# Weight sums one product ahead of the cast that reads them, raw weight tiles of a pair loaded earlier, and the eight parts of z loaded side by side, in a hybrid state-space and attention layer

## The chip, the cores and the metric

The kernel runs on one core of a Trainium2 chip. The metric is the device time of one execution in microseconds (us), as the median over runs. In the traces PE is TensorE (matmuls), DVE is VectorE, ACT is ScalarE, POOL is GpSimd, and SP is SyncE, which here only issues DMAs.

## The reference, cut to what matters

One layer: a projection of 528 tokens (512 and 16 meta tokens), a state-space branch, an attention branch, then sigmoid gates that mix the branches, an output product and a layer norm. The change touches the products of the gates and the entry of the GLU product of the state-space branch:

```python
hf = h.astype(jnp.float32)                                  # 528 x 2048
...
z = jax.nn.gelu(y)                                          # state-space branch, width 1024
hg = z @ w_glu.astype(jnp.float32) + b_glu.astype(jnp.float32)
return hg[..., :SSM_WIDTH] * jax.nn.sigmoid(hg[..., SSM_WIDTH:])
...
gates = jax.nn.sigmoid(hf @ w_gate[layer].astype(jnp.float32) + b_gate[layer].astype(jnp.float32))
mixed = gates[..., :D_MODEL] * y_ssm + gates[..., D_MODEL:] * y_sb
```

## The kernel before

All large products are made in three passes: each float32 operand is split into a high half (a cast on ACT) and a low half (source less high half, a subtraction on DVE, `split_lo`), and `mm3` issues high by high, high by low and low by high. In the trace the high halves of a weight tile are called `whi`, the low halves `wlo`, and a raw tile is 128 x 1024 float32 (512 KB).

Weights go through a pipeline of three functions that count factors. `load_upto` issues the DMA of raw tiles on SP, `prep_upto` makes `whi` and `wlo`, and `slot` runs one factor's matmuls. `slot` for factor c first runs what is left of the product before (`pend`), prepares factors up to c + 2, and then writes eight pieces of three matmuls; ahead of the sixth piece it issues loads up to factor c + 5. Fillers (`schedule`) are pieces of other work that `run_fillers` puts in at a given count of pieces. The order is the order in which this Python runs: the program is recorded under `manual_schedule`, each engine takes its own instructions in that order, and semaphores hold an instruction until its inputs are there and its output buffer is free. `whi` and `wlo` have three buffers each, so those for product x + 2 take the place of those of product x - 1.

**The gates** are made in 16 pairs (`pair(j)`), one for 128 columns of each of the two gates. A pair has four raw tiles, `11`, `12`, `21`, `22` (gate one or two, first or second half of the 2048 input rows), and is computed with seven products in place of eight (Strassen's scheme in Winograd's form): sums of the raw tiles are multiplied with sums of quarters of the input (`T1`, `T2`, `T3`, `t4`, made ahead). Products are numbered 0 to 6 here; their factors are `11`, `s2`, `s1`, `21` (overwritten by 11 - 21), `12`, `s2` (overwritten by 12 - s2) and `22`, with s1 = 21 + 22 and s2 = s1 - 11. The sums are DVE instructions of 128 x 1024. In the kernel before `factor` writes a sum at the place where its product's factor is prepared, right ahead of the cast that reads it; s1 and s2 both stand ahead of the cast for product 1. A product is 24 matmuls of 256 columns. The products accumulate into three PSUM tiles a, b, c; `e0` to `e6` add them up on DVE and apply the sigmoid on ACT, each written at the start of the next slot. b takes products 1, 3 and 6; `e1` reads b after product 1 (`u2`, b + p1), so product 3 can't start before that addition is done.

The raw tiles `11`, `21` and `12` share three buffers, and `22` has two of its own. `11`, `21` and `22` of a pair are issued together, at product 2 of the pair before, and `12` at product 3; what really holds each is its buffer, which the pair before has to release.

**The entry of the GLU product.** z lies in DRAM as eight parts of 128 x 512 (`zd`, 256 KB each). Their high and low halves `zh` and `zl` are needed by all 16 products of the GLU, part kk by piece kk. `load_z(j)` is a filler that issues the DMA into `zt` (one buffer), the cast to `zh` and the subtraction to `zl`; eight of them are placed three pieces apart, from product 4 of the last pair on. Their place in memory is that of `T1` to `T3`, which product 3 of the last pair reads last.

## Time and profile before

| | |
|---|---|
| median of 3 runs | 1505.92 us (1505.59 to 1507.81) |
| the profiled execution, its own time | 1507.89 us |
| its span, first to last instruction | 1506.1 us |
| PE busy | 1440.1 us, 96% |
| DVE busy | 942.0 us, 63% |
| ACT busy | 482.0 us, 32% |
| mean granted clock of PE | 0.988 of full |

The span is what the trace covers; 1.8 us of the execution's own time lie around it. Matmuls are pipelined: one of 256 columns is shown 0.28 us long, but starts follow each other every 0.12 us, so a gap is read from the starts of neighbours. The idle time that a view puts before a matmul is counted from the modelled end of the one before, and is shorter than the delay of its start.

### The profile page before, as it was taken

To read this page: it belongs to the slowest core of one execution; us is meant where nothing else is said; L and a number is where in the kernel's file an instruction comes from. 1 tells how busy PE (TensorE), PEld (TensorE's weight loads), DVE (VectorE), ACT (ScalarE), POOL (GpSimd) and SP (SyncE) were. 2 spreads that over 40 slices of the span, in tenths; PEclk is the share of its full clock that TensorE was granted. 3 is DMA by queue.
4 is the path that set the end of the run, shared out by engine and by line. 5 is a ranking of instruction groups with operands and counts; after the bars stand their busy time and mean duration, and the time that the engine had idled before them with its cause. 6 is when DMAs were issued, how large, how long until landed. Compare 5 with 4: busy or idle time off the path is not lost.

```text
span 1506.1 us, 22031 instructions
## 1 busy us (share of the span) xinstructions
PE 1440.1 (96%) x9040; PEld 1295.2 (86%) x9040; DVE 942.0 (63%) x1397; ACT 482.0 (32%) x764; POOL 48.8 (3%) x95
## 2 busy tenths in 40 slices
PE   7999999999999999998999999996999999999996
PEld 7989999999999898887999999995788888888885
DVE  8887767666767677577666666664454444423357
ACT  5322323233232323234444444433332222221120
POOL 0830000000000000000000000000000000000000
PEclk9999999999999999999999999998899999999998
DMA  7345253434434343462333233233454444474323
GB/s 250 117 129 142 85 141 96 135 105 118 126 114 107 113 116 118 122 219 92 121 131 125 100 133 133 95 124 120 160 150 151 141 151 134 136 208 153 98 98 112
DMA packets 96357, 196.50 MB, mean 130 GB/s; under 512 B 28416, under 2 KB 41984, under 8 KB 95488
## 3 DMA queue, kind: packets, MB, share of 16 engines
q1 hardware_dynamic: 77552, 177.20, 38.5%
q10 hardware_dynamic: 18704, 17.90, 3.5%
q8 instruction: 71, 1.16, 0.3%
q14 instruction: 30, 0.25, 0.1%
HBM read 172.78 MB, written 22.28 MB: 130 GB/s over the span
## 4 chain that ended last, share of the span: by engine, by line
PE 67%; DVE 17%; ACT 8%; issue 5%; DMA 2%; ACTq 0%; SPq 0%; DVEq 0%
PE acc L177 18%; PE acc L178 18%; PE acc L179 18%; ACT whi L171 6%; DVE wlo L96 5%; DVE s L96 4%; PE aux L177 3%; PE aux L179 2%; PE aux L178 2%; DVE u L96 2%; DVE raw L96 1%; DMA zt<-zd 1%; PE aux L818 1%; PE aux L779 1%; PE aux L814 1%
## 5 line engine op out<-in xcount | busy, mean ns | idle before, releaser
L177 PE MATMUL acc<-Xh,whi 128*128 128x256 f32 (+2 forms) x1664 | 520.9, 313 | 6.7 <-ACT whi L277 4.6
L96 DVE TENSOR_TENSOR wlo<-raw,whi 128x1024 fp32r<-128x1024 f32 (+1 forms) x242 | 294.9, 1220 | 362.6 <-ACT whi L171 355.4
L178 PE MATMUL acc<-Xl,whi 128*128 128x256 f32 (+2 forms) x1664 | 515.0, 309 | 2.3 <-DVE Xl L96 2.2
L179 PE MATMUL acc<-Xh,wlo 128*128 128x256 f32 (+2 forms) x1664 | 514.0, 309 | 0.0
L171 ACT CAST whi<-raw 128x1024 fp32r<-128x1024 f32 x238 | 247.7, 1049 | 463.6 <-PE acc L178 311.0
L177 PEld LDWEIGHTS acc<-Xh,whi 128*128 128x128 f32 x1664 | 316.3, 190 | 22.3 <-ACT whi L277 4.6
L178 PEld LDWEIGHTS acc<-Xl,whi 128*128 128x128 f32 x1664 | 316.0, 190 | 17.2 <-DVE Xl L96 3.5
L179 PEld LDWEIGHTS acc<-Xh,wlo 128*128 128x128 f32 x1664 | 315.6, 190 | 15.5
L96 DVE TENSOR_TENSOR wlo<-s,whi 128x1024 fp32r<-128x1024 f32 x48 | 58.8, 1225 | 69.8 <-ACT whi L171 69.8
L171 ACT CAST whi<-s 128x1024 fp32r<-128x1024 f32 x48 | 50.3, 1048 | 89.0 <-DVE s L96 81.5
L177 PE MATMUL acc<-zh,whi 128*128 128x512 f32 x128 | 53.2, 416 | 13.4 <-ACT zh L1180 7.8
L177 PE MATMUL acc<-T3h,whi 128*128 128x256 f32 x128 | 37.4, 292 | 17.4 <-DVE u L96 17.4
L178 PE MATMUL acc<-zl,whi 128*128 128x512 f32 x128 | 52.9, 413 | 0.3 <-DVE zl L96 0.2
L179 PE MATMUL acc<-zh,wlo 128*128 128x512 f32 x128 | 52.2, 408 | 0.0
L179 PE MATMUL acc<-oh,wlo 128*128 128x512 f32 x128 | 49.8, 389 | 0.0
L178 PE MATMUL aux<-wlo,mh 128*128 128x512 f32 x128 | 49.8, 389 | 0.0
L177 PE MATMUL aux<-whi,mh 128*128 128x512 f32 x128 | 49.8, 389 | 0.0
L179 PE MATMUL aux<-whi,ml 128*128 128x512 f32 x128 | 49.8, 389 | 0.0
L178 PE MATMUL acc<-wlo,mh 128*128 128x512 f32 x128 | 49.8, 389 | 0.0
L178 PE MATMUL acc<-sl,whi 128*128 128x512 f32 x128 | 49.8, 389 | 0.0
L178 PE MATMUL acc<-ol,whi 128*128 128x512 f32 x128 | 49.8, 389 | 0.0
L179 PE MATMUL acc<-sh,wlo 128*128 128x512 f32 x128 | 49.8, 389 | 0.0
(274 smaller groups left out, 2310.1 us busy)
## 6 DMA issues: line engine op xcount, KB each, us to landing
raw<-wst SPq DMA_DIRECT2D x238, 512.0 KB
gt<-gtd SPq DMA_DIRECT2D x32, 256.0 KB
xb<-xT SPq DMA_DIRECT2D x16, 264.0 KB
X<-brep SPq DMA_DIRECT2D x8, 512.0 KB
X<-pvd SPq DMA_DIRECT2D x16, 256.0 KB
X<-sd SPq DMA_DIRECT2D x8, 512.0 KB
gtd<-ga ACTq DMA_DIRECT2D x16, 256.0 KB
gtd<-gb ACTq DMA_DIRECT2D x16, 256.0 KB
```

The lines of the kernel that those rows point to most:

```text
L96: eng.tensor_tensor(out, a, b, op)
L171: A.copy(h, t)
L177: PE.matmul(o, ah, bh, start=start, stop=False, **kw)
L178: PE.matmul(o, ah, bl, start=False, stop=False, **kw)
L179: PE.matmul(o, al, bh, start=False, stop=stop, **kw)
L779: PE.matmul(vp[:, g, 0:NK], W["vt"][:, g].rearrange("p r q -> p (r q)"), ut[:, g * NK:g * NK + NK], start=True, stop=True,)
L814: PE.matmul(yp[:, g, 0:SK], W["ot"][:, g].rearrange("p t c -> p (t c)"), hs[:, g * NK + MK - 1:g * NK + MK - 1 + SK], start=True, stop=False,)
L818: PE.matmul(yp[:, g, 0:SK], W["mt"][:, g, :], ut[:, g * NK + MK:g * NK + MK + SK], start=False, stop=True,)
```

## The change

The sums move out of the function that picks a factor. `sums_upto` writes them one product ahead: while factor i is prepared, after its cast and before its low half, it writes the sum that belongs to factor i + 1 (s1 with factor 0, s2 with factor 1, 11 - 21 with factor 2, 12 - s2 with factor 4). `prep_upto` then picks the tile by the table `FACTOR`. The loads of a pair are issued earlier and in another order: `11` and `22` at factor 5 of the pair before (`load_first`), `21` at factor 6 (`load_second`), `12` at factor 1 as before. `load_z` only issues the DMA, into one of eight `zt` buffers, all eight at the start of product 4 of the last pair; `split_z` has the cast and the subtraction, from piece 10 on, two pieces apart. The later loads of `gd`, which use the same tag, get the eight buffers too.

```diff
             else:
-                c = GATES + 4 * pr[0]
-                w = sev.setdefault(pr[0], {})
-                if pr[1] == 0:
-                    w["11"], w["21"] = load_raw(c), load_raw(c + 2)
-                    w["22"] = load_raw(c + 3, sev["p"], "r22", bufs=2)
-                elif pr[1] == 1:
+                n_, x = pr
+                c = GATES + 4 * n_
+                w = sev.setdefault(n_, {})
+                nx = sev.setdefault(n_ + 1, {})
+                if i == GATES:
+                    load_first(w, c)
+                    load_second(w, c)
+                if x == 1:
                     w["12"] = load_raw(c + 1)
+                elif x == 5 and n_ < NSEV - 1:
+                    load_first(nx, c + 4)
+                elif x == 6 and n_ < NSEV - 1:
+                    load_second(nx, c + 4)
...
-    def factor(w, x):
...
+    def load_first(w, c):
+        w["11"] = load_raw(c)
+        w["22"] = load_raw(c + 3, sev["p"], "r22", bufs=2)
+
+    def load_second(w, c):
+        w["21"] = load_raw(c + 2)
+
+    summed = [GATES]
+
+    def sums_upto(f):
+        while summed[0] <= min(f, GATES + 7 * NSEV - 1):
+            n_, x = pair_of(summed[0])
+            w = sev[n_]
+            if x == 0:
+                w["s1"] = sev["p"].tile([P, 1024], F32, tag="s1", name="s1")
+                tt(w["s1"], w["21"], w["22"], ALU.add)
+            elif x == 1:
+                w["s2"] = sev["p"].tile([P, 1024], F32, tag="s2", name="s2")
+                tt(w["s2"], w["s1"], w["11"], ALU.subtract)
+            elif x == 2:
+                tt(w["21"], w["11"], w["21"], ALU.subtract)
+            elif x == 4:
+                tt(w["s2"], w["12"], w["s2"], ALU.subtract)
+            summed[0] += 1
+
+    FACTOR = ("11", "s2", "s1", "21", "12", "s2", "22")
...
-            t = raws.pop(i) if pr is None else factor(sev[pr[0]], pr[1])
+            t = raws.pop(i) if pr is None else sev[pr[0]][FACTOR[pr[1]]]
...
             A.copy(h, t)
+            if GATES - 1 <= i + 1:
+                sums_upto(i + 1)
             split_lo(lo, t, h)
...
-            t = zst["p"].tile([P, S], F32, tag="zt", bufs=1, name="zt")
+            t = zst["p"].tile([P, S], F32, tag="zt", bufs=NT, name="zt")
             SP.dma_start(out=t, in_=zd[j])
+            zst["t", j] = t
+
+        def split_z(j):
+            t = zst.pop(("t", j))
             A.copy(zst["h"][:, j, :], t)
             split_lo(zst["l"][:, j, :], t, zst["h"][:, j, :])
...
-                    schedule([(0, open_z)] + [(1 + 3 * k, lambda k=k: load_z(k)) for k in range(NT)])
+                    schedule([(0, open_z)] + [(0, lambda k=k: load_z(k)) for k in range(NT)]
+                             + [(10 + 2 * k, lambda k=k: split_z(k)) for k in range(NT - 1)] + [(23, lambda: split_z(NT - 1))])
...
-            hold["t2"] = tmpl("zt")
+            hold["t2"] = tmpl("zt", NT)
```

How the instructions stand on DVE from the sum s1 of a pair on, before the change (`raw_7105`, `raw_7107` and `raw_7109` are tiles 11, 21 and 22; `p1`, `u2` and `u3` are the additions of `e6`, `e1` and `e3`):

```order
L96 TENSOR_TENSOR s1_7219<-raw_7107,raw_7109 128x1024
L96 TENSOR_TENSOR s2_7220<-s1_7219,raw_7105 128x1024
L96 TENSOR_TENSOR wlo_7224<-s2_7220,whi_7223 128x1024
L96 TENSOR_TENSOR p1_7049<-p1_7049,acc_7013 128x256
L96 TENSOR_TENSOR wlo_7258<-s1_7219,whi_7257 128x1024
L96 TENSOR_TENSOR raw_7107<-raw_7105,raw_7107 128x1024
L96 TENSOR_TENSOR wlo_7289<-raw_7107,whi_7288 128x1024
L96 TENSOR_TENSOR u2_7316<-acc_7252,p1_7285 128x256
L96 TENSOR_TENSOR wlo_7319<-raw_7142,whi_7318 128x1024
L96 TENSOR_TENSOR s2_7220<-raw_7142,s2_7220 128x1024
L96 TENSOR_TENSOR wlo_7354<-s2_7220,whi_7353 128x1024
L96 TENSOR_TENSOR u3_7384<-acc_7252,p1_7285 128x256
```

The same stretch on DVE with the change (`raw_7041`, `raw_7078` and `raw_7043` are tiles 11, 21 and 22; `raw_6798` is tile 22 of the pair before):

```order
L96 TENSOR_TENSOR s1_7161<-raw_7078,raw_7043 128x1024
L96 TENSOR_TENSOR wlo_7159<-raw_6798,whi_7158 128x1024
L96 TENSOR_TENSOR s2_7193<-s1_7161,raw_7041 128x1024
L96 TENSOR_TENSOR wlo_7191<-raw_7041,whi_7190 128x1024
L96 TENSOR_TENSOR u2_7089<-u2_7089,acc_7015 128x256
L96 TENSOR_TENSOR raw_7078<-raw_7041,raw_7078 128x1024
L96 TENSOR_TENSOR wlo_7224<-s2_7193,whi_7223 128x1024
L96 TENSOR_TENSOR p1_7054<-p1_7054,acc_7014 128x256
L96 TENSOR_TENSOR wlo_7259<-s1_7161,whi_7258 128x1024
L96 TENSOR_TENSOR s2_7193<-raw_7142,s2_7193 128x1024
L96 TENSOR_TENSOR wlo_7293<-raw_7078,whi_7292 128x1024
L96 TENSOR_TENSOR u2_7323<-acc_7253,p1_7290 128x256
```

Each sum now stands one low half earlier than the low half that is made of it: s1 ahead of the low half of the pair before's factor 22, s2 ahead of that of 11, 11 - 21 ahead of that of s2, and 12 - s2 ahead of that of 11 - 21.

On SP around the loads of z, before the change (`DMAHW` is a DMA's semaphore, `DVE`, `PE`, `Pool` and `Activation` those of engines):

```order
L123 DMA raw_10588<-wst 128x1024 [waits DMAHW4_49,DVE_49]
L1179 DMA zt_10617<-zd0_90 128x512 [waits PE_49]
L1179 DMA zt_10630<-zd1_91 128x512 [waits DMAHW6_49,DMAHW5_49,DVE_49]
L123 DMA raw_10637<-wst 128x1024 [waits DMAHW7_49,DMAHW0_49]
L1179 DMA zt_10645<-zd2_92 128x512 [waits DMAHW6_49,DVE_49]
L1179 DMA zt_10664<-zd3_93 128x512 [waits DMAHW1_49,DMAHW0_49,DVE_49]
```

And with the change:

```order
L123 DMA raw_10588<-wst 128x1024 [waits DVE_49]
L1194 DMA zt_10614<-zd0_90 128x512 [waits DMAHW5_49,PE_49]
L1194 DMA zt_10616<-zd1_91 128x512 [waits DMAHW6_49,PE_49]
L1194 DMA zt_10618<-zd2_92 128x512 [waits DMAHW7_49]
L1194 DMA zt_10620<-zd3_93 128x512 [waits DMAHW0_49,PE_49]
L1194 DMA zt_10622<-zd4_94 128x512 [waits DMAHW1_49,Pool_49]
L1194 DMA zt_10624<-zd5_95 128x512 [waits DMAHW2_49,Pool_49]
L1194 DMA zt_10626<-zd6_96 128x512 [waits DMAHW3_49]
L1194 DMA zt_10628<-zd7_97 128x512 [waits DMAHW4_49]
L123 DMA raw_10645<-wst 128x1024 [waits DMAHW5_49,DVE_49]
```

The eight loads of z stand in a row, and none of them waits for DVE, which releases the single buffer in the kernel before.

On ACT at the same place, before the change (`whi_10654` is for the first product of the GLU, `whi_10695` for the second):

```order
L1180 CAST zh_10612<-zt_10630 128x512
L1180 CAST zh_10612<-zt_10645 128x512
L1198 ACTIVATE ga_10652<-acc_10471,bga_217 128x256
L171 CAST whi_10654<-raw_10557 128x1024
L1180 CAST zh_10612<-zt_10664 128x512
L1180 CAST zh_10612<-zt_10679 128x512
L1198 ACTIVATE ga_10652<-u2_10536,bga_217 128x256
L1223 DMA gtd15_129<-ga_10652 128x512
L171 CAST whi_10695<-raw_10588 128x1024
```

And with the change (`whi_10658` and `whi_10697` are those two casts):

```order
L1217 ACTIVATE ga_10656<-acc_10472,bga_217 128x256
L184 CAST whi_10658<-raw_10558 128x1024
L1199 CAST zh_10612<-zt_10614 128x512
L1199 CAST zh_10612<-zt_10616 128x512
L1199 CAST zh_10612<-zt_10618 128x512
L1217 ACTIVATE ga_10656<-u2_10537,bga_217 128x256
L1242 DMA gtd15_129<-ga_10656 128x512
L184 CAST whi_10697<-raw_10588 128x1024
L1199 CAST zh_10612<-zt_10620 128x512
L1199 CAST zh_10612<-zt_10622 128x512
```

The cast for the first GLU product stood behind three casts of z, and now stands ahead of all eight.

## Rows read from the trace of the kernel before

**Rows 1.** Of the page, part 1: busy time of each engine, its share of the span, and instructions.

```profile
PE 1440.1 (96%) x9040; PEld 1295.2 (86%) x9040; DVE 942.0 (63%) x1397; ACT 482.0 (32%) x764; POOL 48.8 (3%) x95
```

**Rows 2.** Who PE waited for, over the whole span: us in total, times, longest.

```profile
PE acc L177 <- DVE u L96: 18.1, 17, 2.3
...
PE acc L179 <- DVE wlo L96: 7.4, 17, 0.8
```

**Rows 3.** Busy time by stretch: the stretch and its length, then busy us (instructions) of PE, PEld, DVE, ACT and POOL, the granted clock of PE, the share of the DMA engines and GB/s. The first row runs from product 3 of the second pair to product 3 of the last, the second lies between the last pair and the GLU, the third and fourth in the GLU.

```profile
714.50:1023.30 308.80, 289.20 (x2353) 283.77 (x2353) 208.21 (x225) 128.65 (x168) 0.00 (x0) 1.00 0.34 120
...
1034.90:1040.60 5.70, 0.13 (x2) 0.02 (x1) 1.42 (x3) 2.19 (x4) 0.00 (x0) 0.82 0.23 81
1040.60:1066.00 25.40, 17.23 (x36) 10.50 (x37) 8.81 (x11) 7.14 (x10) 0.00 (x0) 0.57 0.40 124
1066.00:1145.00 79.00, 79.00 (x350) 65.39 (x349) 36.67 (x43) 27.65 (x36) 0.00 (x0) 1.00 0.49 157
```

**Rows 4.** Timeline of PE: start, us, line, instruction, and in brackets the idle time before it and what ended it. Two rows with 72 matmuls from one to the next, the first matmul of a product 5 and the first of product 1 of the next pair.

```profile
985.03 0.28 PE L177 MATMUL acc<-Xh,whi 128*128 128x256 f32 x1
...
993.67 0.28 PE L177 MATMUL acc<-T2h,whi 128*128 128x256 f32 x1
```

**Rows 5.** Timeline of PE, the waits at products 3 (`T3h`) and 2 (`T1h`) of the pairs, the last row in the last pair.

```profile
714.52 0.35 PE L177 MATMUL acc<-T3h,whi 128*128 128x256 f32 x1 [1.01 <-DVE u L96]
...
732.65 0.39 PE L179 MATMUL acc<-T1h,wlo 128*128 128x256 f32 x1 [0.39 <-DVE wlo L96]
...
736.55 0.35 PE L177 MATMUL acc<-T3h,whi 128*128 128x256 f32 x1 [1.01 <-DVE u L96]
...
1023.27 0.36 PE L177 MATMUL acc<-T3h,whi 128*128 128x256 f32 x1 [1.00 <-DVE u L96]
```

**Rows 6.** Timeline of DVE, from the sum s1 (`s<-raw`) of the third pair to the addition `u2` ahead of its product 3.

```profile
724.15 1.22 DVE L96 TENSOR_TENSOR s<-raw 128x1024 f32<-128x1024 f32 x1
725.40 1.22 DVE L96 TENSOR_TENSOR s<-s,raw 128x1024 f32<-128x1024 f32 x1
727.79 1.23 DVE L96 TENSOR_TENSOR wlo<-s,whi 128x1024 fp32r<-128x1024 f32 x1 [1.17 <-ACT whi L171]
728.93 0.41 DVE L96 TENSOR_TENSOR p<-p,acc 128x256 f32<-128x256 f32 x1
731.37 1.23 DVE L96 TENSOR_TENSOR wlo<-s,whi 128x1024 fp32r<-128x1024 f32 x1 [2.02 <-ACT whi L171]
732.51 1.22 DVE L96 TENSOR_TENSOR raw<-raw 128x1024 f32<-128x1024 f32 x1
734.84 1.23 DVE L96 TENSOR_TENSOR wlo<-raw,whi 128x1024 fp32r<-128x1024 f32 x1 [1.11 <-ACT whi L171]
735.99 0.42 DVE L96 TENSOR_TENSOR u<-acc,p 128x256 f32<-128x256 f32 x1
```

**Rows 7.** Timeline of ACT in the same stretch (ACTq is the issue of a DMA on ACT).

```profile
726.71 1.05 ACT L171 CAST whi<-s 128x1024 fp32r<-128x1024 f32 x1 [1.93 <-DVE s L96]
729.38 0.51 ACT L1198 ACTIVATE gb<-p,bga 128x256 f32<-128x256 f32 x1 [1.62 <-DVE p L96]
729.92 0.33 ACTq L1228 DMA_DIRECT2D gtd<-gb  x1
730.29 1.05 ACT L171 CAST whi<-s 128x1024 fp32r<-128x1024 f32 x1 [0.40 <-ACT gb L1198]
...
733.76 2.00 ACT L171 CAST whi<-raw 128x1024 fp32r<-128x1024 f32 x2 [2.16 <-DVE raw L96]
```

**Rows 8.** Busy time by stretch (columns as in rows 3), 5 us in which the three raw tiles of a pair land.

```profile
715.00:720.00 5.00, 5.00 (x44) 5.00 (x44) 3.62 (x5) 1.17 (x2) 0.00 (x0) 1.00 0.86 313
```

**Rows 9.** Timeline of PE at the first pair: the first matmul of its product 0, and the first of its product 3.

```profile
673.44 0.28 PE L177 MATMUL acc<-Xh,whi 128*128 128x256 f32 x1
...
691.27 0.35 PE L177 MATMUL acc<-T3h,whi 128*128 128x256 f32 x1 [2.26 <-DVE u L96]
```

**Rows 10.** Timeline of PE: the last matmul of the last pair, the first of the GLU, two in its second product, and the first after its 384.

```profile
1034.74 0.28 PE L179 MATMUL acc<-Xh,wlo 128*128 128x256 f32 x1
1040.58 0.80 PE L177 MATMUL acc<-zh,whi 128*128 128x512 f32 x1 [5.57 <-ACT whi L171]
...
1061.12 0.63 PE L177 MATMUL acc<-zh,whi 128*128 128x512 f32 x1
1061.55 0.63 PE L178 MATMUL acc<-zl,whi 128*128 128x512 f32 x1
...
1145.01 0.39 PE L177 MATMUL acc<-sh,whi 128*128 128x512 f32 x1
```

**Rows 11.** Timeline of SP: the issue of the third and the fourth part of z.

```profile
1035.92 0.32 SPq L1179 DMA_DIRECT2D zt<-zd  x1
...
1039.97 0.32 SPq L1179 DMA_DIRECT2D zt<-zd  x1
```

**Rows 12.** Timeline of ACT: the cast of the third part, a sigmoid (`e4`), and the cast for the first GLU product.

```profile
1038.60 0.62 ACT L1180 CAST zh<-zt 128x512 fp32r<-128x512 f32 x1 [3.44 <-DMA zt<-zd]
1039.13 0.47 ACT L1198 ACTIVATE ga<-acc,bga 128x256 f32<-128x256 f32 x1
1039.49 1.03 ACT L171 CAST whi<-raw 128x1024 fp32r<-128x1024 f32 x1
```

**Rows 13.** Timeline of DVE: the low half of the third part.

```profile
1039.25 0.69 DVE L96 TENSOR_TENSOR zl<-zt,zh 128x512 fp32r<-128x512 f32 x1 [3.36 <-ACT zh L1180]
```

More of the change, by code (lines that the diff above doesn't have):

```diff
@@ L139, in load_upto @@
+                if x == 1:
                     w["12"] = load_raw(c + 1)
+                elif x == 5 and n_ < NSEV - 1:
+                    load_first(nx, c + 4)
+                elif x == 6 and n_ < NSEV - 1:
+                    load_second(nx, c + 4)
             issued[0] += 1
-    def factor(w, x):
-        if x == 0:
-            return w["11"]
-        if x == 1:
-            w["s1"] = sev["p"].tile([P, 1024], F32, tag="s1", name="s1")
-            w["s2"] = sev["p"].tile([P, 1024], F32, tag="s2", name="s2")
-            tt(w["s1"], w["21"], w["22"], ALU.add)
-            tt(w["s2"], w["s1"], w["11"], ALU.subtract)
-            return w["s2"]
-        if x == 2:
-            return w["s1"]
-        if x == 3:
-            tt(w["21"], w["11"], w["21"], ALU.subtract)
-            return w["21"]
-        if x == 4:
-            return w["12"]
-        if x == 5:
-            tt(w["s2"], w["12"], w["s2"], ALU.subtract)
-            return w["s2"]
-        return w["22"]
+    def load_first(w, c):
+        w["11"] = load_raw(c)
+        w["22"] = load_raw(c + 3, sev["p"], "r22", bufs=2)
```

## The prediction

> **What bounds the kernel now.** The page comes first: PE is busy for 96% of the span [rows 1], so a gain can only come from the rest, and from stretches in which a busy PE runs at a low clock. The view of who PE waited for names the places: the additions `u` on DVE and the low halves `wlo` at the products of the gates [rows 2]. The stretches then show two bad ones [rows 3]: in the pairs PE is busy for 289.2 of 308.8 us at full clock, and at the entry of the GLU it stands for nearly 5.7 us and then runs 25.4 us at a mean clock of 0.57, the lower of its two levels (1.2 GHz) for most of it. Behind that it is busy throughout.
>
> In the pairs: 72 matmuls take 8.64 us [rows 4], 0.12 us each, so a product takes 2.88 and a pair of seven 20.16. But product 3 starts at 714.52, 736.55 and, 14 pairs after the first of these, at 1023.27 [rows 5]: 22.05 us a pair. The excess of 1.89 us lies at two places of each pair, the low half for product 2 and the addition `u2` that frees b for product 3. DVE and ACT, timeline beside timeline, show why [rows 6, 7]: s1 and s2 stand in a row on DVE (724.15, 725.40), only then can ACT cast s2 (726.71), and DVE stands idle until that cast ends (1.17 us); `p`, the sigmoid of `gb` and the cast of s1 come behind it, each waiting for the one before, then DVE waits again (2.02), makes 11 - 21, waits for its cast (1.11), makes the low half, and only then, at 735.99, comes to `u2`, for which PE stands. DVE isn't too slow, with 208.2 of 308.8 us busy [rows 3]; it and ACT take turns. That is the wait which ends last here.
>
> **The sums, one product earlier.** No instruction is added or dropped; four sums a pair are moved. I lay the new order out on one pair, with T the start of its product 0 and each product 2.88 after the last. Durations are from rows 6 and 7: 1.23 for a sum or a low half (1.14 from start to start where the next doesn't read it), 1.05 for a cast, 0.42 for an addition, 0.51 for a sigmoid, 0.4 for issuing a store, under 0.1 from one engine to another; a product's sums can be read 0.25 after the next product starts, estimated from a matmul's 0.28 against 0.12 [rows 4] and a hand-off. At product 4 (T + 11.5) DVE has `u3` until 12.6, s1 until 13.8, the low half of 22 until 15.4; PE needs that at 17.5. At product 5: s2 until 16.5, the low half of 11 until 17.7, needed at 20.4. At product 6: `u2` until 18.1, 11 - 21 until 19.3; ACT has its sigmoid, the store and the cast of s2 from 19.05 to 20.1, DVE the low half until 21.3, needed at 23.3. At the next product 0 (T now 20.16 later): `p` until 1.5, `gb`, store, cast of s1 until 3.55, low half until 4.8, needed at 6.0. Product 1: 12 - s2 until 5.95, low half of 11 - 21 until 7.15, needed at 8.9. Product 2: `u2` until 7.5, and product 3 wants b at 8.64. So every step is ready 1.0 to 3 us ahead, and the last step ends where the next pair's sequence picks it up: no wait is handed on. PE then sets the pace with 20.16 us. What is next late, by 1.0 to 1.2 us, is `u2` and the low half for product 2.
>
> From product 3 of the first pair to that of the second it is 23.25 us (691.27 to 714.52 [rows 5, 9]), then 14 times 22.05: the gain is 3.1 + 14 × 1.89 = 29.6 us. Bounds: nothing of a wait can be below zero, so 29.6 is the most; the least is the gain if the smaller wait stays (rival below).
>
> **The first pair.** Its product 3 starts 17.83 us after its product 0 [rows 9] in place of 8.64, 9.2 us late; DVE is then still splitting the input sums. The three sums for it now fall ahead, into the last products before, where DVE has slack; of what stands ahead of `u2`, s1 and s2 go (2.45) with the wait for the cast behind them (1.17 [rows 6]), and 11 - 21 comes ahead of another low half (1.22): 2.4 us. Bounds 0 and 9.2; I take 2.4, since the splits of the input remain on both engines.
>
> **The raw tiles.** `11`, `22` and `21` keep their buffers, so the pair before still sets when they start: `11` after 11 - 21, which is now at T - 0.9, `21` after the low half at T + 7.15. Three tiles of 512 KB land within 5 us at 313 GB/s [rows 8], 1.7 us each; a part of z of half the size comes 2.68 us after its issue (1035.92 to 1038.60 [rows 11, 12]), of which 0.84 is its transfer at that rate. By these `21` is there at 7.15 + 1.8 + 1.7 = 10.7; s1 reads it at 12.6. The earlier loads cost nothing, covered by 1.9 us and by 2.1 more ahead of the low half. On SP nothing else is queued in this stretch.
>
> **z side by side.** Before, one buffer makes a ring: load (2.68 from issue to cast), cast 0.62, low half 0.69, next issue (1039.97 after 1035.92 [rows 11 to 13]), 4.05 us for a part. The cast for the first GLU product is queued on ACT behind three parts (1039.49 [rows 12]), PE stands until 1040.58, and as the parts come slower than PE takes them, it stops again and its clock falls: 0.43 between starts at 1061 [rows 10]. From the end of the last pair (1034.86) to the end of the 384 matmuls at 1145.01 are 110.2 us; at full clock they follow each other every 79.0 / 350 = 0.226 us [rows 3], 86.7 in all. The excess is 23.5 us.
>
> With the change, on a clock that starts with product 4 of the last pair: eight issues of 0.32 [rows 11] end by 3.5; 2.1 MB at 313 GB/s take 6.7, so the parts land from 2.8 to about 9. ACT: `ga` 3.1 to 3.6, the GLU's first cast until 4.6, `zh` 0 to 2 until 6.2; DVE: low half until 5.8, `zl` 0 to 2 until 7.6, `u2` until 8.0. Then `ga`, store and the second cast until 10.0, `zh` 3 to 7 until 12.7; DVE makes that low half until 11.2, `zl` 3 until 11.85, and one more every 0.6. PE starts the GLU at 8.64 and takes a part every 0.68; it wants `zl` 3 at 10.9. One wait of 1.0 us is left, and the later parts keep ahead. Waits of that size in the pairs leave the clock at 1.00 [rows 3, 5]. The gain is 22.5; bounds 17 (second rival) and 23.5.
>
> The Trainium skill (DMA: Bandwidth & Descriptors, section "Queues, rings and completion order") says that a DMA engine takes the descriptors of one ring in ring order, though a later one may complete first. By that the parts land nearly in turn, as taken here; no row of this case shows two parts in flight. If the rule didn't hold here, the second rival would be the sum.
>
> **The sum.** 29.6 + 2.4 + 22.5 = 54.5 us. The profiled execution took 1507.89 us (span 1506.1), 2.0 above the median of 1505.92; against its own time that gives 1453.4, and against the median 1451.4. Behind the GLU PE is busy throughout, so what is won there is handed on to the end.
>
> **Rivals.** *One wait a pair stays.* The spare of 1.0 to 1.2 us at product 2 and `u2` hangs on five hand-offs in a row (`u2`, `ga`, cast, low half, `p`, `gb`, cast, low half). If each takes 0.25 more than the rows show, or a sum waits for its tile, the smaller wait stays. Of the idle time it is 0.39 beside 1.01 [rows 5], so of the 1.89 a pair 0.53, × 15 = 7.9 us: 1459. For it speaks how DVE idles behind ACT [rows 6]; against it that every step was laid out with those hand-offs.
>
> By the Trainium skill (TensorE: Matmul & The Clock Gate, section "Architectural detail: the array is 16× 32×32, not 1× 128×128") ScalarE and VectorE take their queues strictly in order, so a sum written ahead of another product's low half would hold it up. The trace agrees: the low half at 731.37 waits 2.02 us for its cast, and 11 - 21 stands behind it [rows 6].
>
> *The parts of z land together.* If the eight share the DMA engines evenly, the first is there at 8.5, not at 2.8. Then `zh` 0 to 2 end at 10.2, `u2`, `ga`, store and the second cast at 13.3, its low half at 14.5, `zl` 3 at 15.2: 4.3 us of waits in place of 1.0, and a clock at its lower level for some 11 matmuls, 0.2 us more each (by 1034.9 to 1066 [rows 3, 10]): 5.6 more, 1457.
>
> *The change does half of what it says.* If the place of the parts isn't free before product 6 is done, the loads are as late as now: 32 us of gain alone, 1474. The order speaks against it: the first load waits for PE, whose last reader of `T3` is product 3.
>
> *Slower.* DVE is stopped in the middle of its queue by s1 waiting for tile `21`, and the low half of 22, `u2` and all behind it come late in each pair. To use up 54.5 us and 3 more, that is 3.8 us a pair beyond the spare: `21` would have to land at 14.7 + 3.8 = 18.5, 11.3 us after its buffer is free. From there on the change loses; three such tiles land in 5 us [rows 8].
>
> **How the numbers follow.** The forecast 0.73, one wait a pair 0.10, z together 0.11, half of it 0.03, slower 0.03 (of which 0.01 within the bound of 0.2%, about what a measurement of this kernel can tell from no change). The forecast's own bounds are 1448 (2 us more of the first pair, no wait at the GLU) and 1455 (0.2 us a pair left). With it alone 0.73 would be inside; the range goes up to 1460, over the two cases at 1457 and 1459, and leaves out the rest. Faster 0.97, same 0.01, slower 0.02.
>
> **What would show it.** Pairs 20.2 us apart with no wait for `u` or `wlo` behind the first; DVE idle for casts only where PE doesn't wait; s1 never waiting for a DMA; PE waiting at most once, for `zl`, in the first GLU product, at a granted clock of 1.00 from 1002 to 1090; the GLU's 384 matmuls in 88 us. Wrong it would be if a wait for `u` at product 3 stayed, or if DVE idled for `raw`, or if the clock fell at the GLU.

## The result, and the profile after

The changed kernel takes 1458.67 us (median of 4 runs, 1457.13 to 1459.57), the kernel before 1506.51 in the runs beside it (1505.59 to 1507.81): a ratio of 0.9681, 95% interval [0.9664, 0.9698]. The profiled execution took 1458.41 us against 1507.89.

Part 1 of the page of the changed kernel, which answers to [rows 1], shows the instruction counts of before on every engine; only PE's busy time moves by more than 5 us, as it no longer runs at a low clock at the GLU:

```profile
PE 1425.7 (98%) x9040; PEld 1291.6 (89%) x9040; DVE 937.2 (64%) x1397; ACT 482.8 (33%) x764; POOL 49.3 (3%) x95
```

Who PE waited for in the changed kernel (us in total, times, longest), beside [rows 2]. By this view no `u` is left, `wlo` fell from 17 waits to three, and one `zl` is there. The three waits for `wlo` and the three for `whi` of L184 all stand at the first pair:

```profile
PE acc L192 <- ACT whi L292: 4.7, 1, 4.7
PE acc L192 <- ACT whi L184: 3.9, 3, 1.5
PE acc L194 <- DVE wlo L96: 3.6, 3, 1.8
...
PE acc L193 <- DVE zl L96: 0.7, 1, 0.7
```

Busy time by stretch in the changed kernel, columns as in [rows 3]: the pairs from product 3 of the second to that of the last, the rest of the last pair, and the GLU. In the pairs PE is busy without a gap, at the GLU 0.74 us are missing, and the granted clock is 1.00 in all three, so always the upper of the two levels (2.4 GHz):

```profile
714.20:996.40 282.20, 282.20 (x2354) 282.20 (x2354) 205.56 (x224) 130.11 (x168) 0.00 (x0) 1.00 0.39 130
996.40:1008.00 11.60, 11.60 (x99) 11.60 (x98) 6.66 (x9) 5.98 (x9) 0.00 (x0) 1.00 0.81 281
1008.00:1096.00 88.00, 87.26 (x386) 71.91 (x385) 43.57 (x52) 33.50 (x45) 0.00 (x0) 1.00 0.49 159
```

Timeline of PE in the changed kernel: product 3 of the second pair, of the last pair, the first matmul of the GLU, its one wait, and the first matmul behind the GLU. They answer to [rows 5, 10].

```profile
714.26 0.28 PE L192 MATMUL acc<-T3h,whi 128*128 128x256 f32 x1
...
996.50 0.28 PE L192 MATMUL acc<-T3h,whi 128*128 128x256 f32 x1
...
1008.02 0.40 PE L192 MATMUL acc<-zh,whi 128*128 128x512 f32 x1
...
1011.23 0.50 PE L193 MATMUL acc<-zl,whi 128*128 128x512 f32 x1 [0.74 <-DVE zl L96]
...
1096.17 0.39 PE L192 MATMUL acc<-sh,whi 128*128 128x512 f32 x1
```

From the second pair to the last it is now (996.50 - 714.26) / 14 = 20.16 us a pair, and the GLU takes 88.15 in place of the 110.2 that the prediction counted.

At the entry of the GLU SP issued the first load of z at 995.19 and the other seven from 999.45 on, right behind product 3 of the last pair, and the first three casts ran on ACT without a wait. Timelines of SP and ACT in the changed kernel:

```profile
995.19 7.43 SPq L1194 DMA_DIRECT2D zt<-zd  x8
```

```profile
1003.77 1.66 ACT L1199 CAST zh<-zt 128x512 fp32r<-128x512 f32 x3
```

One stretch became longer: the entry of the pairs. In it DVE splits the input sums `T1` to `T3` (made from `xb`), and s1 of the first pair now stands among them. Timelines of the changed kernel: first DVE,

```profile
664.93 1.23 DVE L96 TENSOR_TENSOR s<-raw 128x1024 f32<-128x1024 f32 x1 [3.35 <-DMA raw<-wst]
666.08 1.22 DVE L96 TENSOR_TENSOR wlo<-raw,whi 128x1024 fp32r<-128x1024 f32 x1
...
673.11 0.42 DVE L96 TENSOR_TENSOR xb<-xb 128x256 f32<-128x256 f32 x1 [3.09 <-DMA xb<-xT]
```

then SP, with the three raw tiles of the first pair, tile 12, and the input loads behind it,

```profile
655.24 1.38 SPq L123 DMA_DIRECT2D raw<-wst  x3
658.89 1.11 SPq L1151 DMA_DIRECT2D xb<-xT  x2
667.33 0.33 SPq L123 DMA_DIRECT2D raw<-wst  x1
667.70 9.32 SPq L1151 DMA_DIRECT2D xb<-xT  x6
```

then PE, from the last matmul ahead of the pairs to product 3 of the first pair, where [rows 9] have 17.83 us from product 0 to product 3 and product 0 without a wait:

```profile
674.39 0.39 PE L194 MATMUL acc<-Xh,wlo 128*128 128x512 f32 x1
676.17 0.39 PE L192 MATMUL acc<-Xh,whi 128*128 128x256 f32 x1 [1.39 <-ACT whi L184]
...
678.52 0.58 PE L194 MATMUL acc<-Xh,wlo 128*128 128x256 f32 x1 [1.85 <-DVE wlo L96]
...
694.03 0.36 PE L192 MATMUL acc<-T3h,whi 128*128 128x256 f32 x1 [1.00 <-ACT whi L184]
```

The last of these waits is put down to a cast, but the cast that ends there (693.00 + 1.04) is the one for product 5. What frees product 3 is most likely `u2`: it ends at 693.89, 0.14 ahead of the matmul, the same distance as in the kernel before (735.99 + 0.42, then 736.55 [rows 5, 6]). So one wait for `u2` is left, at the first pair, where `u2` is late like the rest of the entry. On DVE:

```profile
693.47 0.42 DVE L96 TENSOR_TENSOR u<-acc,p 128x256 f32<-128x256 f32 x1
```

In the kernel before the same low half on DVE, and then tile 12 and the input loads on SP, stand here:

```profile
660.66 1.23 DVE L96 TENSOR_TENSOR wlo<-raw,whi 128x1024 fp32r<-128x1024 f32 x1
```

```profile
661.91 0.33 SPq L123 DMA_DIRECT2D raw<-wst  x1
662.28 9.26 SPq L1136 DMA_DIRECT2D xb<-xT  x6
```

So the links are: s1 stands 3.35 us for its raw tile; the low half of factor 95 (the last ahead of the pairs) stands behind it in DVE's queue and starts at 666.08; it releases the buffer into which tile 12 is to be loaded; SP holds that load until 667.33, and the input loads stand behind it, 5.4 us later than before (0.9 of it is a lateness that SP already has at the three raw tiles, issued from 655.24 on here and from 654.35 on before; last section); the next sums on DVE wait 3.09 for `xb`; the cast for product 0 stands behind the `T` casts on ACT (675.08 in place of 669.60); PE stands 1.39 us, and 1.85 more for the low half that s2 was put ahead of.

**Where the 49.5 us between the two profiled executions come from:** pairs from product 3 of the first to the GLU, 343.59 before and 313.99 after, 29.6; GLU, 110.15 (from [rows 10] and the end of the last pair) and 88.15, 22.0; from the last matmul ahead of the pairs (673.22 before, 674.39 after) to product 3 of the first, 18.05 and 19.64, a loss of 1.6; ahead of that 1.2 lost in code that is the same in both; behind the GLU 0.7 less. The 1.2 is PE's clock in the first stage (last section).

### The profile page after: what moved, and what is told of

It is laid out like the page before. It is cut to its first block, busy times and chain, and to the rows that moved or that the text cites. A ratio compares the mean times of both kernels' runs of the same rounds, so it can differ in the third digit from the quotient of the medians.

```text
span 1456.6 us, 22024 instructions
## 1 busy us (share of the span) xinstructions
PE 1425.7 (98%) x9040; PEld 1291.6 (89%) x9040; DVE 937.2 (64%) x1397; ACT 482.8 (33%) x764; POOL 49.3 (3%) x95
## 4 chain that ended last, share of the span: by engine, by line
PE 90%; DVE 5%; DMA 2%; issue 1%; ACT 1%; SPq 0%; DVEq 0%; ACTq 0%
PE acc L192 26%; PE acc L193 26%; PE acc L194 26%; PE aux L192 3%; PE aux L194 2%; PE aux L193 2%; PE aux L794 1%; PE aux L833 1%; PE aux L829 1%; DVE wlo L96 1%; PE aux L940 1%; DVE Xl L96 1%; DMA raw<-wst 1%; ACT whi L184 1%; PE aux L765 0%
## 5 line engine op out<-in xcount | busy, mean ns | idle before, releaser
L184 ACT CAST whi<-raw 128x1024 fp32r<-128x1024 f32 x238 | 249.4, 1049 | 445.9 <-PE acc L193 328.1
L184 ACT CAST whi<-s 128x1024 fp32r<-128x1024 f32 x48 | 50.3, 1048 | 41.8 <-PE acc L193 28.1
L193 PE MATMUL acc<-zl,whi 128*128 128x512 f32 x128 | 49.9, 390 | 0.7 <-DVE zl L96 0.7
L192 PE MATMUL acc<-zh,whi 128*128 128x512 f32 x128 | 49.8, 389 | 0.0
L192 PE MATMUL acc<-sh,whi 128*128 128x512 f32 x128 | 49.8, 389 | 0.0
L192 PE MATMUL acc<-oh,whi 128*128 128x512 f32 x128 | 49.8, 389 | 0.0
L192 PE MATMUL acc<-whi,mh 128*128 128x512 f32 x128 | 49.8, 389 | 0.0
L194 PE MATMUL acc<-whi,ml 128*128 128x512 f32 x128 | 49.8, 389 | 0.0
```

The costliest lines, as they stand in the source:

```text
L184: A.copy(h, t)
L192: PE.matmul(o, ah, bh, start=start, stop=False, **kw)
L193: PE.matmul(o, ah, bl, start=False, stop=False, **kw)
L194: PE.matmul(o, al, bh, start=False, stop=stop, **kw)
```

## The experiments

The column "entry" of the table is the time from the last matmul ahead of the pairs to product 3 of the first pair, which leaves out most of what an execution lost before it. It is read from one execution of each: where the entry is the same program, it is 18.05 and 17.53 (before, e2), and 19.20 to 19.93 (changed, e3, e4, e8), so differences under 0.7 us are not told apart. "Pairs and GLU" runs from that product 3 to the first matmul behind the GLU. Ratios are to the kernel before, run beside each.

| | median, us | ratio | entry, us | pairs and GLU, us |
|---|---|---|---|---|
| before | 1506.51 | | 18.05 | 453.74 |
| changed | 1458.67 | 0.9681 [0.9664, 0.9698] | 19.64 | 402.14 |
| e1, s1 behind the low half | 1455.23 | 0.9653 [0.9638, 0.9668] | 15.37 | 402.02 |
| e2, z alone | 1487.44 | 0.9871 [0.9855, 0.9888] | 17.53 | 432.32 |
| e3, sums alone | 1479.17 | 0.9817 [0.9803, 0.9832] | 19.20 | 422.98 |
| e4, loads as before | 1458.73 | 0.9679 [0.9665, 0.9694] | 19.68 | 402.25 |
| e5, one more sum a pair | 1458.70 | 0.9685 [0.9669, 0.9701] | 20.15 | 402.29 |
| e6, two more | 1477.51 | 0.9809 [0.9795, 0.9824] | 20.63 | 421.79 |
| e7, e1 and earlier parts of z | 1454.18 | 0.9652 [0.9636, 0.9668] | 15.52 | 402.02 |
| e8, changed again | 1457.35 | 0.9675 [0.966, 0.9689] | 19.93 | 402.08 |
| e9, tile 12 later | 1455.56 | 0.9648 [0.9634, 0.9661] | 16.58 | 402.12 |
| e10, 11 - 21 and 12 - s2 later | 1455.92 | 0.9654 [0.9641, 0.9667] | 17.56 | 402.10 |
| e11, three edits together | 1453.28 | 0.9637 [0.9621, 0.9654] | 14.10 | 402.20 |
| e12, they where they were | 1480.17 | 0.9816 [0.9802, 0.983] | 19.01 | 423.63 |

**e1: s1 of the first pair behind the low half of factor 95, not ahead of it**

```diff
             A.copy(h, t)
-            if GATES - 1 <= i + 1:
+            if GATES <= i:
                 sums_upto(i + 1)
             split_lo(lo, t, h)
+            if i == GATES - 1:
+                sums_upto(GATES)
```

> The changed kernel, but for the first pair alone the sum s1 stands behind the low half of the factor before it in place of ahead. Theory (s1 waits on DVE for its raw tiles, and the low half queued behind it releases the buffer of tile 12 late, for which SP holds the next loads of the input): the 3.4 us wait of DVE before s1 remains, but the low half is made before it, the input loads behind tile 12 are issued some 5 us earlier, product 0 of the first pair doesn't wait for its cast, and product 3 of the first pair starts 18 to 19 us after the end of the product before the pairs, in place of 19.4; in all 3 to 5 us faster than the changed kernel, near 1454.5. Rival (the three sums of 1.2 us are themselves too much for DVE in this stretch): within 0.5 us of the changed kernel, near 1458.

Measured: 1455.23 us, and an entry of 15.37 us. Timeline of DVE in this run, and then of SP:

```profile
663.40 1.23 DVE L96 TENSOR_TENSOR wlo<-raw,whi 128x1024 fp32r<-128x1024 f32 x1
666.69 1.23 DVE L96 TENSOR_TENSOR s<-raw 128x1024 f32<-128x1024 f32 x1 [2.06 <-DMA raw<-wst]
```

```profile
664.65 0.33 SPq L123 DMA_DIRECT2D raw<-wst  x1
665.03 9.16 SPq L1153 DMA_DIRECT2D xb<-xT  x6
```

s1 still waits for its tile, but nothing that others need stands behind it any more: tile 12 is issued 0.02 us after the low half ends, the input loads right after, and product 0 starts without a wait. The loss at the entry was the place of one instruction, not its work: the sum is still made, and the entry is 4.3 us shorter than in the changed kernel.

**e2 and e3: one part of the change alone.** e2 is the kernel before with the edits of `load_z`, `split_z` and their schedule, e3 the changed kernel with those taken back. Of e3, the schedule:

```diff
...
-                    schedule([(0, open_z)] + [(0, lambda k=k: load_z(k)) for k in range(NT)]
-                             + [(10 + 2 * k, lambda k=k: split_z(k)) for k in range(NT - 1)] + [(23, lambda: split_z(NT - 1))])
+                    schedule([(0, open_z)] + [(1 + 3 * k, lambda k=k: load_z(k)) for k in range(NT)])
...
```

> The kernel before with the change of the z parts alone. Theory (terms add): 22 us less than before, near 1484.5, with one wait of about 1 us for zl in the first product of the GLU. Rival (the z parts only come in time because DVE and ACT are freed by the earlier sums): a loss of 5 us or more of that, 1490.

> The changed kernel with the old loads and splits of z. Theory: pairs 20.16 us apart, 29.6 us won there and 1.6 lost at the first pair, near 1478.5; the GLU's 384 matmuls take 109 to 111 us as before. Rival (the pairs gain only what the z parts don't take back): over 1483.

Measured: 1487.44 and 1479.17 us. Who PE waited for in e2 has the waits of the pairs as before (and 0.3 us for `zh` in place of 7.8); in e3 it is the other way round:

```profile
PE acc L177 <- DVE u L96: 18.1, 17, 2.3
PE acc L179 <- DVE wlo L96: 7.3, 17, 0.8
```

```profile
PE acc L192 <- ACT zh L1195: 7.9, 4, 2.6
PE acc L192 <- ACT whi L184: 6.5, 3, 4.2
```

By the column of pairs and GLU the z part is worth 21.4 us and the sums 30.8, together 52.2, and the whole change 51.6: the two parts add up, within the 0.7 of one such reading. The median of e2 is 20.0 us below the kernel before beside it (1507.40), 2 less than expected; its four runs span 2.7 us, and the profiled one, at 1485.21, is the lowest of them.

**e4: the raw loads as before,** all three of a pair at product 2 of the pair before it, the sums one product earlier as in the changed kernel:

```diff
-                n_, x = pr
-                c = GATES + 4 * n_
-                w = sev.setdefault(n_, {})
-                nx = sev.setdefault(n_ + 1, {})
-                if i == GATES:
-                    load_first(w, c)
-                    load_second(w, c)
-                if x == 1:
+                c = GATES + 4 * pr[0]
+                w = sev.setdefault(pr[0], {})
+                if pr[1] == 0:
+                    w["11"], w["21"] = load_raw(c), load_raw(c + 2)
+                    w["22"] = load_raw(c + 3, sev["p"], "r22", bufs=2)
+                elif pr[1] == 1:
                     w["12"] = load_raw(c + 1)
-                elif x == 5 and n_ < NSEV - 1:
-                    load_first(nx, c + 4)
-                elif x == 6 and n_ < NSEV - 1:
-                    load_second(nx, c + 4)
```

> The changed kernel with the raw tiles of a pair issued at their old places (11, 21, 22 together, 22 behind 21). Theory (the buffers, not the place in the program, set when a load starts, and s1 has 2 us to spare): tile 22 comes some 1.7 to 5 us later, DVE waits for it at s1 for 0 to 1 us a pair, PE doesn't: same time within 1 us, near 1458.5. Rival (the earlier loads are needed for the sums to be early): PE waits 0.5 us or more in each pair, 1466 or more.

Measured: 1458.73 us, the same as the changed kernel, with the same entry. DVE now does wait for the tile at s1, in three of the 15 sums s1 behind the first, by 0.61 to 0.82 us, and PE has no wait in these pairs. The first of them, in the second pair for the third:

```profile
717.25 1.23 DVE L96 TENSOR_TENSOR s<-raw 128x1024 f32<-128x1024 f32 x1 [0.61 <-DMA raw<-wst]
```

The earlier loads bring nothing that can be measured, and they cost nothing.

**e5 and e6: one and two needless sums a pair,** of the size of the others, ahead of the low half for product 3 and so ahead of `u2` (e6 has the added line twice). They change no result, as s1 is not read behind them:

```diff
             elif x == 4:
                 tt(w["s2"], w["12"], w["s2"], ALU.subtract)
+                tt(w["s1"], w["12"], w["22"], ALU.add)
```

> The changed kernel with one sum of 128 x 1024 more on DVE in each pair, ahead of the low half of 11 - 21 and so of u2; it writes a tile that nothing reads any more, so the output stays the reference's. Theory (u2 and the low half for product 2 have a spare of about 1.2 us, and a sum takes 1.14 from start to start): used up, but not passed: at most 0.2 us a pair, 1458 to 1462. Rival (the pairs are free of waits because DVE's total work fits, with a third of its time free, and not because of this one spare): no change, and none with two sums either.

> The same with two such sums. Theory: u2 comes 2 x 1.14 - 1.2 = 1.1 us late, and PE waits for u at product 3 of each pair: 16 x 1.1 = 17 us more, near 1475. Rival (total work of DVE counts, 17.4 of 20.2 us a pair): no change, 1458 to 1460.

Measured: 1458.70 and 1477.51 us. One is free. Two cost 19.65 us in pairs and GLU (421.79 against 402.14). In e6 product 3 of every pair waits again for `u2`, here in the third; behind the second pair they come 21.37 us apart ((1015.72 - 716.47) / 14), 1.21 more than in the changed kernel:

```profile
737.82 0.36 PE L194 MATMUL acc<-T3h,whi 128*128 128x256 f32 x1 [0.97 <-DVE u L96]
```

Two sums take 2 × 1.14 = 2.28, so the spare in front of `u2` is 2.28 - 1.21 = 1.1 us, which fits that one sum of 1.14 is free. DVE's free time as a whole, the rival in both, would have carried the second sum too.

**e7: e1, and all parts of z two pieces earlier** (the fourth then falls ahead of `u2` of the last pair).

```diff
-                             + [(10 + 2 * k, lambda k=k: split_z(k)) for k in range(NT - 1)] + [(23, lambda: split_z(NT - 1))])
+                             + [(8 + 2 * k, lambda k=k: split_z(k)) for k in range(NT)])
```

> The first experiment's place for s1 of the first pair, and the splits of z at pieces 8 + 2k in place of 10 + 2k, so that four of them stand ahead of u2 and of the second GLU cast, not three. Theory: zl of the fourth part is there in time and the wait of 1 us in the first GLU product goes: 4 to 5 us less than the changed kernel, near 1454, the fastest version. Rival (the wait moves to another part, or u2 comes late and with it the sigmoid and the second cast): no less than the first experiment.

Measured: 1454.18 us, within the scatter of e1. The wait for `zl` didn't go, it moved from the fourth part to the fifth, and stands at 0.67 us:

```profile
1005.91 0.50 PE L195 MATMUL acc<-zl,whi 128*128 128x512 f32 x1 [0.67 <-DVE zl L96]
```

**e8: the changed kernel again.**

> The changed kernel itself once more, beside the others on the same chip, for the comparison of a few us: 1457 to 1460, with the first pair's product 0 late in its profile as in the first one (theory: a wait in the program's order, so in every run).

Measured: 1457.35 us; the entry is 19.93 us, with a wait of 1.68 for the cast of product 0. The loss at the entry belongs to the kernel, not to one execution.

**e9: tile 12 of the first pair behind the input loads on SP,** s1 where the change put it:

```diff
             i = issued[0]
             pr = pair_of(i)
+            if i == GATES + 1 and f == i:
+                break
```

> The changed kernel with one thing moved: the load of raw tile 12 of the first pair is issued one product slot later, so that on SP it stands behind the input loads of the entry product instead of ahead of them; s1 of the first pair stays ahead of the low half of factor 95, as in the changed kernel. Theory (the link is SP's queue: s1 waits for tile 21, the low half behind it is late, tile 12's buffer comes free late, and the input loads queue behind that load): the input loads are issued within 1 us of where the kernel before issues them, the T casts are on time, product 0 starts no later than 2.2 us after the end of the product ahead of it, and the time falls by about 3 us, to 1454 to 1456 us. Rival (the 3.3 us that VectorE itself loses waiting for tile 21 ahead of the low half is enough): the half of factor 95 and the entry sums stay late, and the time stays within 1 us of the changed kernel, 1457.5 to 1459.5 us.

Measured: 1455.56 us. DVE loses as much at s1 as in the changed kernel (3.43 us), but the input loads don't stand behind tile 12 any more. SP in this run:

```profile
655.51 1.38 SPq L123 DMA_DIRECT2D raw<-wst  x3
659.16 12.04 SPq L1153 DMA_DIRECT2D xb<-xT  x6
671.25 0.43 SPq L123 DMA_DIRECT2D raw<-wst  x1
```

Product 0 starts without a wait (674.58, 0.23 behind the matmul ahead). So the wait on DVE did most of its harm through SP's queue: the entry is 16.58 us, 3.1 of the 4.3 us that e1 wins. The 1.2 that remain against e1 were not traced further.

**e10: fewer sums ahead.**

```diff
+            if pr is not None:
+                sums_upto(i)
             t = raws.pop(i) if pr is None else sev[pr[0]][FACTOR[pr[1]]]
...
             if GATES - 1 <= i + 1:
-                sums_upto(i + 1)
+                sums_upto(i + 1 if pair_of(i + 1) and pair_of(i + 1)[1] < 2 else i)
```

> The changed kernel with two of the four moved sums put back: 11-21 and 12-s2 are again made just ahead of the half of a product that reads them, while s1 and s2 stay one product earlier. Theory (s1 and s2 head the chain of sums that the pair waited for; 11-21 and 12-s2 have room where they stood): TensorE waits at most 0.3 us a pair for sums, and the time is 1459 to 1463 us. Rival (every sum moved counts alike, so half of the moves brings half of the pairs' gain of 29.6 us): about 1473 us.

Measured: 1455.92 us, faster than both theories, but the expectation describes another kernel: 11 - 21 and 12 - s2 went back by one product only, not by two, and stand one low half ahead of their own. (In the changed kernel they stand two ahead of their own, s1 three and s2 one; that each sum stands one low half earlier, as the part on the change puts it, holds for s2 alone.) What it tells: 11 - 21 behind `p` falls into a time in which DVE waits for the cast of s1 anyway, so it is early enough there, the pairs have no wait, and the entry is 2.1 us shorter than in the changed kernel. That one sum less then stands ahead of the low halves that are late there would explain it, but was not tried by itself. Timeline of DVE in the third pair:

```profile
722.95 0.41 DVE L96 TENSOR_TENSOR p<-p,acc 128x256 f32<-128x256 f32 x1
723.27 1.22 DVE L96 TENSOR_TENSOR raw<-raw 128x1024 f32<-128x1024 f32 x1
725.38 1.23 DVE L96 TENSOR_TENSOR wlo<-s,whi 128x1024 fp32r<-128x1024 f32 x1 [0.89 <-ACT whi L186]
726.60 1.23 DVE L96 TENSOR_TENSOR wlo<-raw,whi 128x1024 fp32r<-128x1024 f32 x1
727.95 0.42 DVE L96 TENSOR_TENSOR u<-acc,p 128x256 f32<-128x256 f32 x1
```

**e11: e1, e10 and six parts of z ahead of `u2` of the last pair.**

```diff
-                             + [(10 + 2 * k, lambda k=k: split_z(k)) for k in range(NT - 1)] + [(23, lambda: split_z(NT - 1))])
+                             + [(10 + k if k < 6 else 6 + 2 * k, lambda k=k: split_z(k)) for k in range(NT)])
```

> Three edits of the changed kernel together: s1 and s2 alone are made one product earlier (as in e10), s1 of the first pair stands behind the low half of factor 95 (as in e1), and six in place of three casts and low halves of z stand ahead of u2 of the last pair's product 5 (the other two behind the cast for the second GLU product). Theory (the wait for the fourth low half comes from standing behind u2, its sigmoid and the cast for the second GLU product, and VectorE and ScalarE have room for six parts ahead of them): no wait for zl is left, which is 1.0 us; the first pair takes 14 to 15.1 us from the end of the product ahead to its product 3; together 1452.5 to 1454.5 us. Rival (u2, moved 1.8 us later by three more low halves, makes the second GLU product late in place of the first): the wait goes from zl to whi or acc at the second product, and the time is 1454.5 to 1456.

Measured: 1453.28 us, the lowest median of all, though its runs (1451.32 to 1455.47) overlap those of e1 and e7, and the shortest entry, 14.10 us. A wait for `zl` of 0.52 us is left, now at the seventh part; the expected end of it was wrong. It always stands at the first part behind the cast for the second GLU product.

**e12: what e10 was to be.**

```diff
+            if pr is not None:
+                sums_upto(i - 1)
             t = raws.pop(i) if pr is None else sev[pr[0]][FACTOR[pr[1]]]
...
-            if GATES - 1 <= i + 1:
+            if pair_of(i + 1) and pair_of(i + 1)[1] < 2:
                 sums_upto(i + 1)
```

> What e10 was meant to be: s1 and s2 stay one product earlier, while 11-21 stands behind the low half of s1 and directly ahead of its own low half, and 12-s2 directly ahead of its own, as in the kernel before (in e10 both stood one place earlier than that). Worked out from the profiled run of e10: there 11-21 and the low half of s1 come one after the other, the low half of 11-21 ends at 727.83, u2 at 728.37, and product 3 wants b at 730.58; if 11-21 (1.22) stands behind the low half of s1 (ending at 725.5 then, since its cast decides) the cast of 11-21 (1.05), its low half (1.23) and u2 (0.42) follow, so that u2 ends at about 729.7 to 730.4. Theory (s1 and s2 alone carry the gain of the pairs): no wait for u at product 3 or at most 0.2 us a pair, 1455 to 1459 us. Rival (11-21 must be ahead too, since sum, cast and low half then stand in a row behind the cast of s1): waits for u at product 3 in all 15 pairs of 0.5 us or more, 1464 us or more.

Measured: 1480.17 us. The rival holds, and by more than its bound. DVE in the third pair, and the matmul that waits:

```profile
731.34 1.22 DVE L96 TENSOR_TENSOR wlo<-s,whi 128x1024 fp32r<-128x1024 f32 x1 [2.02 <-ACT whi L186]
732.48 1.22 DVE L96 TENSOR_TENSOR raw<-raw 128x1024 f32<-128x1024 f32 x1
734.82 1.23 DVE L96 TENSOR_TENSOR wlo<-raw,whi 128x1024 fp32r<-128x1024 f32 x1 [1.12 <-ACT whi L186]
735.96 0.41 DVE L96 TENSOR_TENSOR u<-acc,p 128x256 f32<-128x256 f32 x1
```

```profile
736.52 0.36 PE L194 MATMUL acc<-T3h,whi 128*128 128x256 f32 x1 [1.01 <-DVE u L96]
```

From product 3 of the second pair (715.06) to that of the last (1015.65) it is 21.47 us a pair, 1.31 more than PE needs. Sum, cast and low half stand in a row behind the cast of s1, with waits of 2.02 and 1.12 as in [rows 6], and `u2` ends at 736.37, just ahead of the matmul that it frees. My working had the low half of s1 start earlier without 11 - 21 ahead of it; but it stands 2.4 us behind `p` in e10 and in e12 alike, since the cast of s1 decides. Moving s1 and s2 alone is worth 22.05 - 21.47 = 0.58 us a pair, and it takes away just the waits for the low half at product 2: of the 17 waits for `wlo` two are left, both in the first pair, while the 17 for `u` stay.

```profile
PE acc L194 <- DVE u L96: 16.7, 17, 1.0
...
PE acc L196 <- DVE wlo L96: 2.6, 2, 1.8
```

The other 1.31 come with 11 - 21 and 12 - s2 out of their places between two casts. Which of these two carries more isn't told apart.

## Why the prediction was right, and where not

The forecast of 1451.4 was 7.3 us below the median. The median lies within the range, but by luck: the forecast's own bounds were 1448 and 1455, and 1458.67 is inside only because the range was stretched to 1460 over two rivals at 1457 and 1459, neither of which happened. That it comes within 0.4 us of the rival "one wait a pair stays" is chance. Without the 4.0 us that the first pair missed by, the forecast's own bounds would have held. The mechanism of the two large terms was right. The terms, in their order:

- **The pairs, 29.6 us: 29.6 measured,** with PE at 20.16 us a pair and no gap. Four sums were laid out, and e12 shows that the two that follow s1 and s2 carry 1.31 of the 1.89 us of a pair, and s1 and s2 the other 0.58; the prediction's split by idle time, 0.53 for the smaller wait, comes close to that. The layout put the spare at `u2` and the low half for product 2 at 1.0 to 1.2 us; e6 gives 1.1. The rival "one wait a pair stays" is refuted: behind the first pair no pair has a wait.
- **z, 22.5 us: 22.0 measured,** with the one wait that was predicted, for the fourth `zl`, 1.14 from start to start in place of 0.23. In e7 and e11 it moved to the first part that stands behind the cast for the second GLU product: a place in a queue, not a size. The half microsecond that is missing is the pace of the matmuls: the 374 matmuls from that wait on take 84.94 us, 0.227 each, where the prediction took 0.226 from a count of 350 that includes two already running at the start of the stretch. No cast of z waited for a DMA. The first three ended 6.1 us after the start of product 4 (999.38), not 10.2, so "the parts of z land together" is refuted as it was priced. "The change does half of what it says" is refuted too: the loads were issued right behind product 3, not behind product 6. By the Trainium skill (DMA: Bandwidth & Descriptors, section "Queues, rings and completion order") a DMA engine takes the descriptors of one ring in ring order; no row here shows in which order the parts landed, only that none was late.
- **The first pair, 2.4 us gained: 1.6 lost,** which is outside the term's bounds of 0 and 9.2. This is the step that failed. The prediction took what stands ahead of `u2` of the first pair and said that "the three sums for it now fall ahead, into the last products before, where DVE has slack". DVE had slack there, but it is a queue: s1 waits in it for its raw tile, and what stands behind it waits too. The price of a raw tile was worked out for the pairs only ("the earlier loads cost nothing", "on SP nothing else is queued in this stretch"), where both hold (e4). At the entry neither does: three tiles and the input loads are in flight together, and s1 is the first to want them. e1 removes the harm by the place on DVE; e9, with the sum left where it is, removes all but 1.2 us of it by the place on SP. So most of the harm needs both links. In e1 the entry is 2.7 us shorter than before, so the 2.4 was sized about right for a first pair whose input is on time.
- **The last rival named the right mechanism in the wrong place:** s1 in the middle of DVE's queue, waiting for tile `21`. It was priced for every pair, where it doesn't happen, and it happens once. The prediction weighed the strict order of the queues against the low halves of the pairs with the Trainium skill (TensorE: Matmul & The Clock Gate, section "Architectural detail: the array is 16× 32×32, not 1× 128×128"), by which ScalarE and VectorE take their instructions strictly in order. The trace agrees at the entry as well: the low half of factor 95, which starts 5.4 us later behind s1 (666.08 against 660.66), is the case of that rule which cost time.
- **The rest of the 7.3 us:** 4.0 from the first pair, 0.5 from z (half a microsecond of pace, as above), 0.5 net from the stages that the change doesn't touch (1.2 lost ahead, 0.7 less behind), and 2.2 because the profiled execution before was 2.0 above its median and the one after 0.3 below its own.

What stays open: the waits that the entry still has (in the changed kernel six of 0.76 to 1.85 us, at products 0 to 3) were not taken away one by one, nor was 11 - 21 tried without 12 - s2.

## What to carry to other kernels

Where two engines take turns (sum on one, cast on the other, low half on the first), look for the step that stands between two casts and move that one out; moving the sums at the head of the row alone brought 0.58 of 1.89 us a pair. Before an instruction is written earlier, ask at every place where the loop is entered, not only in the steady state, whether its input is there, what is queued behind it, and which buffer that releases to which other queue. A load that waits for a buffer belongs behind the loads that wait for nothing.

## What the runs showed of the hardware

Executions differ by up to 3.6 us ahead of all that the change touches, and the granted clock shows where. Busy time by stretch from 100 to 120 us, columns as in [rows 3], in the kernel before, the changed kernel, and e11:

```profile
100.00:120.00 20.00, 17.06 (x145) 16.25 (x145) 17.43 (x23) 5.03 (x12) 0.00 (x0) 1.00 0.19 58
```

```profile
100.00:120.00 20.00, 17.57 (x136) 16.75 (x136) 17.40 (x23) 4.71 (x10) 0.00 (x0) 0.91 0.22 63
```

```profile
100.00:120.00 20.00, 17.55 (x126) 16.73 (x125) 17.40 (x23) 4.56 (x9) 0.00 (x0) 0.85 0.21 61
```

PE stands 2.4 to 2.9 us in this stretch in all of them. In some executions the clock is then at its lower level (1.2 GHz) for a while (mean 0.91 and 0.85), in others never (1.00), by which e11 gets 19 matmuls less done there than the kernel before. The last matmul ahead of the pairs then starts at 674.39 and 675.82 in place of 673.22; in e7, whose clock was 1.00 in that stretch, it starts at 672.60, and in e1 and e3, at 0.86, at 676.15 and 676.19. It is not the edit: e8 is the changed kernel again, and in its execution the clock was 1.00 there and that matmul started at 673.37, 1.0 earlier than in the first. Differences of 2 us between variants are thus read from a stretch behind it, as the table of the experiments does, not from single executions.
